# A sub-norm's scale spread over partitions: by way of DRAM, or by products with the identity

## The chip, the cores and the metric

One core of one Trainium2 chip runs the whole kernel. The metric is the device time of one execution in microseconds (us), as the median of several runs. The engines are named as in the profile: PE is TensorE, with PEld its weight loads, DVE is VectorE, ACT is ScalarE, POOL is GpSimd, and SP is SyncE, which issues the weight transfers. Each engine works through its own instructions in the order in which they stand.

## The reference, cut to what matters

Two layers run over 256 tokens of width 2048 in float32: a layer whose mixer is a convolution, then one whose mixer is a differential attention with 16 heads, each followed by a feed-forward part with a short convolution. The change lies in the attention, between the value product of a head and the output projection:

```python
a = p[:, :, 0] - lam * p[:, :, 1]
return jnp.einsum('bhqk,bkhe->bqhe', a.astype(v.dtype), v)
...
o = _rmsnorm(o, subln_g) * (1.0 - lambda_init)
return o.reshape(B, S, D_MODEL) @ w_o
```

So each head's output of 128 channels is divided, token by token, by the root of the mean of its squares, before it is multiplied by the learned gain and goes into `w_o`.

## The kernel before, in words

Activations lie with channels on the 128 partitions and the 256 tokens along the free dimension. A matrix product takes weights from DRAM in tiles of 128 x 1024 (512 KB), one tile a step (L183, `run`). Each tile is split by `split_w` into a rounded part `hi` (ACT, L150) and the rest `lo` (DVE, L152, or POOL), and PE multiplies `hi` with both parts of the activation (L226, 512 columns) and `lo` with the first (L227, 256 columns). That is one pair of products; a step of the query/key and output products is eight such pairs. The tiles are split four steps ahead of their use, and up to five raw tiles are on their way.

Work that follows a product is put off by a number of steps with `self.at(delay, fn)`, so that other products lie between a piece of work and what it waits for. The order on each engine comes from the program order, as shifted by a scheduler of the language, and is fixed when the kernel is built.

The attention (`attention`) runs over 16 heads. Before every fourth head stands a group of eight steps that makes the values of four heads (`v_group`, L774 to L776). Then come four steps for each head's query and key (`qk_post`, with the addition L256, the multiplication L795, the splits L263 and L264 and POOL's copy G at L801). Scores (L819, L822) and softmax follow two steps later, transposes (L847) four after that, the value product (`av`, L856 to L859) three after that. `av` writes the PSUM tile `o`; ACT copies it to SBUF and squares it (L862, L864). Two steps later `subln` sums the squares over the channels on PE (L274, `chan_sums`), which leaves one value for each token with the tokens on partitions; DVE scales them (L285) and POOL takes the power -0.5 (L286, tile `c`).

To multiply the head's output, this value must stand in every partition with the tokens along the free dimension. Heads 0 to 13 do that by way of DRAM: L878 writes the 256 values to the DRAM tile `rd`, and L879 reads them back into all 128 partitions, as the SBUF tile `M`. Both are issued from ACT's queue, and L879 can only be issued when L878's transfer has landed. Three steps later `subln2` multiplies (DVE, L886) and splits the result for the output projection (L267, L268). Heads 14 and 15 use `rows` instead (L280): two products with the identity matrix, whose stationary side is the column `c` repeated 128 times, write the values into all partitions of a PSUM tile, `o` or `t`.

The PSUM tag `o` is one bank with one buffer, `t` likewise, `s` has two; the large products use `pp`. A tile of a tag with one buffer can be written only when the reader of the tile before it has finished.

The output projection takes the heads' outputs as its inner dimension, 16 products of 128 channels for each pair of output tiles. The last head's products are held back for the first pairs.

Of the kernel before, what the change touches and what calls it, by code (L numbers as in the profile page):

```python
# [8 lines left out]
F32 = mybir.dt.float32  # L9
# [5 lines left out]
P = 128  # L15
S = 256
# [9 lines left out]
class Cfg:  # L26
    """Shapes; everything follows from the model width and the FFN width."""

    def __init__(self, d, f, kc=4):
        self.D, self.F = d, f  # L30
        self.KT = d // P
        self.FT = f // P
        self.H = d // (2 * HD)
        self.KC = kc
        self.NW = kc * 256
        self.kcs = [(i, kc) for i in range(0, self.KT, kc)]
        full = self.KT // 2
        first = self.FT % full or full
        self.chunks = [(0, first)] + [(i, full) for i in range(first, self.FT, full)]
        self.VK = kc // 2  # L40
        self.NA, self.NB = self.KT + self.KT // 2 + 1, 8
        # taps of the 31-tap convolution that go to the tensor engine, in fours, by channel tile
        self.G = [2] * (self.KT - 5) + [3, 3, 5, 6, 0]
        # the last tile's taps go there one by one
        self.ND = 18
# [16 lines left out]
class Builder:  # L62
# [25 lines left out]

    # temporaries; a tag's tiles are handed out in program order, so what runs late has tags of its own
    def b2(self, tag, dt=F32):  # L90
# [21 lines left out]

# [1 line left out]
    def act_tile(self, dt=F32R):  # L114
# [18 lines left out]

# [1 line left out]
    def load_w(self):  # L135
# [20 lines left out]
    def ahead(self, i):  # L156
        """weight tiles up to i split, some more on their way"""
        N = len(self.W)
        while self.ns < min(N, i + 1):
            while self.np_ < min(N, self.ns + 5):  # L160
                self.load_w()
            self.split_w()
# [38 lines left out]

# [1 line left out]
    def pair(self, wsrc, off, ksub, src, post, lo="v", pre=None, held=None, merged=False, halves=None):  # L203
        """halves(): two banks of [P, 512] instead of one tile of two;
        ksub: [(k0, nk)]; src(k) -> activation slot; held: a list that takes the last k instead of a step"""
        nc = self.nc
# [43 lines left out]
    def summed(self, ps):  # L250
        """main + correction halves -> [P, 2, S] in SBUF"""
        nc = self.nc
        cs = self.b2("E")
        nc.scalar.copy(cs, ps[:, :, S:])  # L254
        t = self.b2("E")
        nc.vector.tensor_tensor(t, ps[:, :, 0:S], cs, ALU.add)  # L256
        return t

    def split_act(self, dst, src, scale=None, num=None):
        """dst [P, 2, S] f32r <- hi and lo of src*scale (scale: [P, 1] pointer, or num: an exact number)"""  # L260
        nc = self.nc
        if scale is None and num is None:
            nc.scalar.copy(dst[:, 0, :], src)  # L263
            nc.vector.tensor_tensor(dst[:, 1, :], src, dst[:, 0, :].bitcast(F32), ALU.subtract)  # L264
        else:
            sc = num if scale is None else scale
            nc.scalar.activation(dst[:, 0, :], src, AF.Copy, scale=sc)  # L267
            nc.vector.scalar_tensor_tensor(dst[:, 1, :], src, sc, dst[:, 0, :].bitcast(F32), ALU.mult, ALU.subtract)  # L268

# [1 line left out]
    def chan_sums(self, ps, srcs):  # L271
# [5 lines left out]
    def rows(self, ps, col):  # L277
        """ps [P, S] <- col [P, 2] with tokens along the free dim, in every partition"""
        for t in range(2):
            self.nc.tensor.matmul(ps[:, t * P:(t + 1) * P], col[:, t:t + 1].to_broadcast([P, P]), self.ident,  # L280
                                  start=True, stop=True)
# [5 lines left out]

# [1 line left out]
    def new_norm(self, gname, goff, final=False):  # L289
# [49 lines left out]
    def norm_rows(self, st):  # L339
        ps = self.psx("o", [P, S])  # L340
        self.rows(ps, st["rc"])
        st["rows"] = ps
        if st["final"]:
            # the vector engine reads one copy in PSUM, GpSimd another by way of SBUF
            ps = self.psx("t", [P, S])
            self.rows(ps, st["rc"])
        st["rstd"] = self.const.tile([P, S], F32, tag="rstd", name=self.nm("rstd"), bufs=2)
        self.nc.scalar.copy(st["rstd"], ps)
# [6 lines left out]

# [1 line left out]
    def x_add(self, ps, pr, bias=None, merged=False):  # L357
# [66 lines left out]

# [1 line left out]
    def conv_module(self, nin, nout):  # L426
        c, a = self.c, self.a
# [5 lines left out]
        def post(i, ps):  # L433
# [11 lines left out]
            if i == KT - 1:  # L445
                self.at(0, lambda: last_taps(u, dgl))
                return
            # four shifted copies of 32 channels each, by way of DRAM: [(shift, channel), block, token]
            g = c.G[i]
# [11 lines left out]
            if i == 0:  # L461
                # diagonal weights of the last tile's taps on the tensor engine
                for j in range(0, c.ND, 4):
                    t = self.b2("Y" if j < 16 else "A").rearrange("p a (b s) -> p (a b) s", b=2)[:, :min(4, c.ND - j), :]
                    n = t.shape[1]
                    nc.gpsimd.tensor_tensor(t, self.ident.unsqueeze(1).to_broadcast([P, n, P]),
                                            self.col("cw", (KT - 1) * CK + j, n).unsqueeze(2).to_broadcast([P, n, P]), ALU.mult)
                    dgl.extend(t[:, x, :] for x in range(n))
# [10 lines left out]
        def last_taps(u, dgl):  # L479
            """the last tile: taps on both engines at once, in sums of their own"""  # L480
            i = KT - 1
# [24 lines left out]
        def tap_step(n=6):  # L506
            """some taps on the vector engine, two tiles by turns so that none waits for the one before it"""
            while chains and n > 0:
# [21 lines left out]
        def shift(c0):  # L530
            """per-token shift: the mean of the first tile; it cancels in the normalisation"""
            ps = self.psx("o", [P, S])
# [45 lines left out]
        def layernorm():  # L578
# [44 lines left out]
            with self.tc.manual_schedule(engines={ET.DVE, ET.Activation, ET.Pool}):  # L623
# [8 lines left out]
                for i in range(KT):  # L632
                    # a vector-engine pair is normalised at least one pair ahead of its use
                    while todo and 2 * todo[0][0] + todo[0][1] <= i + 2:
                        norm(*todo.pop(0))
                    act(i)
                    if todo and i >= 1:
                        norm(*todo.pop(0))
                    low(i)
# [17 lines left out]

# [1 line left out]
    def ffn(self, layer, nin, nout, begin=None):  # L659
# [57 lines left out]

# [1 line left out]
    def attn_setup(self):  # L719
        """relative bias by distance, one sheared copy per query row in DRAM; lambda"""  # L720
        nc, c, a = self.nc, self.c, self.a
# [27 lines left out]
    def attention(self, nin, nout):  # L749
# [63 lines left out]
        def scores(h, q, k, qk):  # L813
            bm = bias(h)
            ps = [self.psx("s", [P, 2, S]) for _ in range(2)]
            # the first 128 queries see the first 128 keys only: one float32 product costs less than three of 256 columns
            comp = [slice(cc * HD, (cc + 1) * HD) for cc in range(2)]
# [49 lines left out]
        def subln(h, o, sq):  # L867
# [3 lines left out]
            self.rsqrt_cols(rc, ps[:, 0:4:2], 1.0 / P)  # L871
            if h >= H - 2:
                self.at(2, lambda: subln2(h, o, rc, None))
                return
            # to every partition by way of DRAM
            rd = self.dr.tile([S], F32, tag="rd", name=self.nm("rd"), bufs=3)
            rr = self.b1("M")
            nc.scalar.dma_start(rd.rearrange("(t p) -> p t", p=P), rc)  # L878
            nc.scalar.dma_start(rr, rd.unsqueeze(0).to_broadcast([P, S]))  # L879
            self.at(3, lambda: subln2(h, o, rc, rr))  # L880

        def subln2(h, o, rc, rr):
            if rr is None:
                rr = self.psx("t" if h == H - 1 else "o", [P, S])
                self.rows(rr, rc)
            nc.vector.tensor_tensor(o, o, rr, ALU.mult)  # L886
# [64 lines left out]
def _onehot(np):  # L951
    """bucket of each distance key - query = j - 255"""
    oh = np.zeros((NB, 384), np.float32)
# [8 lines left out]
def layout(cfg, inp):  # L962
    """host side: repacking only"""
    import numpy as np
# [79 lines left out]
```

## Time and profile before

| | |
|---|---|
| median of 3 runs | 2394.99 us (2393.94 to 2396.80) |
| span of the profiled execution | 2415.1 us |
| PE busy | 2255.2 us, 93% of the span |
| DVE busy | 1667.8 us, 69% |
| ACT busy | 1201.8 us, 50% |
| POOL busy | 283.3 us, 12% |
| DMA | 419.02 MB, mean 174 GB/s |

The profile is of one execution, and its span runs from the first to the last instruction; it is 20.1 us longer than the median of the runs, which were taken without a profile. No other time of that execution is given. A busy share is an average over stages with different limits, so the stretch where the attention runs, about 1138 to 1606 us of the span, has to be read by itself. A wait names the instruction that ended it. The granted clock is a share of 2.4 GHz: 1.00, or 0.50, which is 1.2 GHz.

### The profile page before, as it was taken

Reading aid. Unit: us, or ns where it says so; the run is one execution under the profiler, and the core shown is the slowest. Engines: PE = TensorE matmul, PEld = TensorE weight load, DVE = VectorE, ACT = ScalarE, POOL = GpSimd, SP = SyncE. Lnnn points to the kernel's source line nnn. Section 1 sums busy time; section 2 is a strip of 40 time slices with the busy share of each in tenths; the row PEclk is TensorE's granted clock in tenths of the full one; section 3 lists DMA queues with packets and bytes.
Section 4 is the critical chain, followed back from the end, with each engine's and each line's share of the span. In section 5 each row is a group of like instructions: output and inputs, shape, how many; then the busy total and the mean of one; then the engine's idle time right before and its main releaser. Section 6 shows DMA issues by size and latency. Waiting matters only on the chain. (4 is left out here: it accounts for less than half of the span.)

```text
span 2415.1 us, 34577 instructions
## 1 busy us (share of the span) xinstructions
PE 2255.2 (93%) x13238; PEld 1968.0 (81%) x13238; DVE 1667.8 (69%) x2539; ACT 1201.8 (50%) x1788; POOL 283.3 (12%) x189
## 2 busy tenths in 40 slices
PE   6999799899999999999978776889999999999998
PEld 6888688788888888888867665778888888888887
DVE  5888874777767677778646363667777767676774
ACT  4333363655545455556534343455555555454554
POOL 5678410000000000001101000110000000000002
PEclk8999899899999999999988888899999999999999
DMA  6766267666666666666655545555666666666663
GB/s 227 196 186 189 78 197 185 191 187 191 189 189 186 190 190 188 190 185 190 181 98 142 121 124 104 132 155 183 188 188 186 191 186 189 191 185 191 185 190 105
DMA packets 132711, 419.02 MB, mean 174 GB/s; under 512 B 18208, under 2 KB 34112, under 8 KB 132544
## 3 DMA queue, kind: packets, MB, share of 16 engines
q1 hardware_dynamic: 110736, 398.30, 55.7%
q10 hardware_dynamic: 21808, 18.51, 4.0%
q8 instruction: 104, 1.70, 0.3%
q14 instruction: 63, 0.52, 0.1%
HBM read 409.27 MB, written 7.47 MB: 173 GB/s over the span
## 5 line engine op out<-in xcount | busy, mean ns | idle before, releaser
L226 PE MATMUL pp<-act,hi 128*128 128x512 f32 x3902 | 1393.8, 398 | 28.8 <-DVE E L256 13.2
L227 PE MATMUL pp<-act,lo 128*128 128x256 f32 x3902 | 1101.6, 282 | 0.0
L150 ACT CAST hi<-raw 128x1024 fp32r<-128x1024 f32 x752 | 787.4, 1049 | 550.2 <-issue 172.2
L152 DVE TENSOR_TENSOR lo<-raw,hi 128x1024 fp32r<-128x1024 f32 x686 | 844.0, 1231 | 260.9 <-ACT hi L150 259.9
L226 PEld LDWEIGHTS pp<-act,hi 128*128 128x128 f32 x3902 | 739.1, 189 | 193.3 <-DVE E L256 13.5
L227 PEld LDWEIGHTS pp<-act,lo 128*128 128x128 f32 x3902 | 745.0, 191 | 10.3 <-issue 0.7
L226 PE MATMUL pp<-actb,hi 128*128 128x512 f32 x856 | 309.7, 399 | 0.0
L227 PE MATMUL pp<-actb,lo 128*128 128x256 f32 x856 | 241.8, 283 | 0.0
L217 PE MATMUL pp<-act,hi 128*128 128x256 f32 x1088 | 210.1, 295 | 11.3 <-ACT act L267 6.2
L321 POOL TENSOR_TENSOR ssq<-ssq,Z 128x512 f32<-128x512 f32 x24 | 35.5, 1481 | 1530.9 <-ACT Z L317 1530.8
L217 PEld LDWEIGHTS pp<-act,hi 128*128 128x128 f32 x1088 | 178.9, 201 | 20.7 <-DVE act L268 6.3
L226 PEld LDWEIGHTS pp<-actb,hi 128*128 128x128 f32 x856 | 162.3, 190 | 38.9 <-issue 0.6
L256 DVE TENSOR_TENSOR E<-pp,E 128x512 f32<-128x512 f32 x104 | 72.0, 692 | 164.2 <-ACT E L254 163.8
L254 ACT COPY E<-pp 128x512 f32<-128x512 f32 x104 | 60.9, 586 | 231.5 <-PE pp L224 170.6
L152 POOL TENSOR_TENSOR lo<-raw,hi 128x1024 fp32r<-128x1024 f32 x66 | 159.3, 2432 | 59.1 <-ACT hi L150 54.0
L227 PEld LDWEIGHTS pp<-actb,lo 128*128 128x128 f32 x856 | 163.2, 191 | 0.3 <-issue 0.2
L217 PE MATMUL pp<-act,lo 128*128 128x256 f32 x544 | 158.4, 291 | 2.8 <-DVE lo L152 2.8
L370 ACT COPY E<-pp 128x512 f32<-128x512 f32 x109 | 64.1, 588 | 168.7 <-PE pp L224 161.1
L677 DVE SCALAR_TENSOR_TENSOR Y<-fpad,prm,Y 128x256 f32<-128x256 f32 x352 | 147.0, 480 | 0.0
L372 DVE TENSOR_TENSOR x<-pp,x 128x512 f32<-128x512 f32 x101 | 69.9, 692 | 88.6 <-ACT E L370 88.1
L674 ACT ACTIVATE Y<-fpad,prm 128x256 f32<-128x256 f32 x176 | 96.3, 595 | 48.2 <-DVE fpad L670 48.2
L513 DVE SCALAR_TENSOR_TENSOR s<-cpad,cprm,s 128x256 f32<-128x256 f32 x214 | 97.5, 482 | 23.3 <-PE s L475 21.0
(219 smaller groups left out, 1912.8 us busy)
## 6 DMA issues: line engine op xcount, KB each, us to landing
raw<-in_w_up_dram SPq DMA_DIRECT2D x352, 512.0 KB, 3.9
raw<-in_w_down_dram SPq DMA_DIRECT2D x176, 512.0 KB, 3.9
raw<-in_w_in_dram SPq DMA_DIRECT2D x64, 512.0 KB, 4.5
raw<-in_w_qk_dram SPq DMA_DIRECT2D x64, 512.0 KB, 4.3
raw<-in_w_out_dram SPq DMA_DIRECT2D x32, 512.0 KB, 4.2
raw<-in_w_v_dram SPq DMA_DIRECT2D x32, 512.0 KB, 3.7
raw<-in_w_o_dram SPq DMA_DIRECT2D x32, 512.0 KB, 3.8
R<-ud ACTq DMA_DIRECT2D x44, 130.0 KB, 5.3
```

The costliest lines, as they stand in the source:

```text
L150: nc.scalar.copy(hi[:, :n], raw[:, :n])
L152: eng.tensor_tensor(lo[:, :n], raw[:, :n], hi[:, :n].bitcast(F32), ALU.subtract)
L217: nc.tensor.matmul(ps[:, 0:S], w[:, kk, cs], xt[:, x, :], start=(k == first and n == 0), stop=(k == last and n == 2))
L226: nc.tensor.matmul(*main, start=(k == first), stop=False)
L227: nc.tensor.matmul(*corr, start=False, stop=False)
L254: nc.scalar.copy(cs, ps[:, :, S:])
L256: nc.vector.tensor_tensor(t, ps[:, :, 0:S], cs, ALU.add)
L370: nc.scalar.copy(cs, ps[:, :, S:])
L372: nc.vector.tensor_tensor(x, ps[:, :, 0:S], x, ALU.add)
L513: nc.vector.scalar_tensor_tensor(acc, u[:, j:j + S], self.col("cw", i * CK + j), acc, ALU.mult, ALU.add)
L674: nc.scalar.activation(y[:, j, :], u[:, j, FK - 1:], AF.Identity, scale=self.col("fw", ch * FK + FK - 1), bias=self.col("fb", ch))
L677: nc.vector.scalar_tensor_tensor(y[:, j, :], u[:, j, q:q + S], self.col("fw", ch * FK + q), y[:, j, :], ALU.mult, ALU.add)
```

## The change

All 16 heads take the way that heads 14 and 15 took: the two transfers and the tiles `rd` and `M` are gone from `subln`, and `subln2` makes the scale with `rows`, always two steps after the sums.

```diff
             self.rsqrt_cols(rc, ps[:, 0:4:2], 1.0 / P)
-            if h >= H - 2:
-                self.at(2, lambda: subln2(h, o, rc, None))
-                return
-            # to every partition by way of DRAM
-            rd = self.dr.tile([S], F32, tag="rd", name=self.nm("rd"), bufs=3)
-            rr = self.b1("M")
-            nc.scalar.dma_start(rd.rearrange("(t p) -> p t", p=P), rc)
-            nc.scalar.dma_start(rr, rd.unsqueeze(0).to_broadcast([P, S]))
-            self.at(3, lambda: subln2(h, o, rc, rr))
-
-        def subln2(h, o, rc, rr):
-            if rr is None:
-                rr = self.psx("t" if h == H - 1 else "o", [P, S])
-                self.rows(rr, rc)
+            self.at(2, lambda: subln2(h, o, rc))
+
+        def subln2(h, o, rc):
+            rr = self.psx("t" if h == H - 1 else "o", [P, S])
+            self.rows(rr, rc)
             nc.vector.tensor_tensor(o, o, rr, ALU.mult)
```

The diff also drops comments and docstrings elsewhere; they move line numbers only (L886 is L877 in the changed kernel). The order of instructions on the engines shifts too. The names in the rows below are tiles with buffer numbers: `rd` and `M` as above, `E` a sum of two halves, `hi`, `lo` and `raw` weight tiles, `Y` the split query and key, `O` a head's output or its squares, `c` the column of scales, `at` and `au` the transposed weights of the attention, `act` and `actb` activations, `pp`, `o` and `s` PSUM tiles.

ACT, where head 0's scale is ready, about where the second value group begins; first the kernel before:

```order
L878 DMA rd_11689<-c_11685 128x2x1
L254 COPY E_11715<-pp_11568 128x512
L150 CAST hi_11762<-raw_11594 128x1024
L879 DMA M_11690<-rd_11689 128x256
L150 CAST hi_11828<-raw_11660 128x1024
L263 CAST Y_11720<-E_11717 128x256
L263 CAST Y_11721<-E_11717 128x256
L862 COPY O_11756<-o_11751 128x256
L864 ACTIVATE O_11758<-o_11751 128x256
L267 ACTIVATE act_11786<-O_11590,subg 128x256
```

and the changed one:

```order
L254 COPY E_11711<-pp_11568 128x512
L150 CAST hi_11765<-raw_11594 128x1024
L150 CAST hi_11827<-raw_11660 128x1024
L263 CAST Y_11716<-E_11713 128x256
L263 CAST Y_11717<-E_11713 128x256
L862 COPY O_11752<-o_11747 128x256
L864 ACTIVATE O_11754<-o_11747 128x256
```

The two transfers are gone from between the copy and the casts, and with L879 the point where ACT had to see L878's transfer landed.

DVE at the same place, before:

```order
L152 TENSOR_TENSOR lo_11763<-raw_11594,hi_11762 128x1024
L886 TENSOR_TENSOR O_11590<-O_11590,M_11690 128x256
L152 TENSOR_TENSOR lo_11829<-raw_11660,hi_11828 128x1024
L264 TENSOR_TENSOR Y_11720<-E_11717,Y_11720 128x256
L264 TENSOR_TENSOR Y_11721<-E_11717,Y_11721 128x256
```

and changed:

```order
L152 TENSOR_TENSOR lo_11766<-raw_11594,hi_11765 128x1024
L152 TENSOR_TENSOR lo_11828<-raw_11660,hi_11827 128x1024
L264 TENSOR_TENSOR Y_11716<-E_11713,Y_11716 128x256
L264 TENSOR_TENSOR Y_11717<-E_11713,Y_11717 128x256
L152 TENSOR_TENSOR lo_11853<-raw_11689,hi_11852 128x1024
L264 TENSOR_TENSOR at_3963<-t_11781,at_3963 128x256
L877 TENSOR_TENSOR O_11590<-O_11590,o_11756 128x256
L829 SCALAR_TENSOR_TENSOR Z_11803<-s_11791,bm_11788 128x128
```

The multiplication of head 0's output stands five rows later, behind two more weight splits and three activation splits, and reads the PSUM tile `o` that the identity products write.

PE at the tenants of the bank `o`, in the third value group, with most other products left out (one row of the scores, L819, is kept for the place); before, heads 5, 5, 6, 6 and 7:

```order
L856 MATMUL o_12596<-at_3965,act_11736 128x256
...
L819 MATMUL s_12637<-G_12567 128x128
...
L274 MATMUL o_12689<-ones,O_12603 128x2 x2
...
L856 MATMUL o_12736<-at_3963,act_11737 128x256
...
L274 MATMUL o_12792<-ones,O_12743 128x2 x2
...
L856 MATMUL o_12860<-at_3965,act_11738 128x256
```

and changed, heads 5, 4, 5, 6, 5, 6 and 7:

```order
L856 MATMUL o_12588<-at_3965,act_11732 128x256
...
L819 MATMUL s_12632<-G_12559 128x128
...
L280 MATMUL o_12597<-ident,c_12526 128x128 x2
...
L274 MATMUL o_12684<-ones,O_12595 128x2 x2
...
L856 MATMUL o_12727<-at_3963,act_11733 128x256
...
L280 MATMUL o_12736<-ident,c_12687 128x128 x2
...
L274 MATMUL o_12786<-ones,O_12734 128x2 x2
...
L856 MATMUL o_12850<-at_3965,act_11734 128x256
```

Between a value product and the sums of its own squares now stands the scale of the head before, in the same bank. In the changed order 26, 24, 20, 22, 24 and 20 other products stand in the six gaps.

## Rows read from the trace of the kernel before

**Rows 1.** The page's 40 slices of 60.4 us: PE's busy tenths, granted clock.

```profile
PE   6999799899999999999978776889999999999998
PEclk8999899899999999999988888899999999999999
```

**Rows 2.** Windows: length, busy us of each engine, PEclk, DMA share, GB/s.

```profile
1138.00:1212.00 74.00, 74.00 (x412) 62.44 (x411) 50.78 (x94) 40.20 (x76) 8.73 (x9) 1.00 0.60 181
1296.00:1332.00 36.00, 36.00 (x211) 30.38 (x209) 26.66 (x63) 18.41 (x44) 4.04 (x7) 1.00 0.55 142
1212.00:1324.00 112.00, 88.74 (x440) 73.17 (x439) 57.67 (x125) 44.65 (x98) 9.41 (x12) 0.86 0.52 122
1210.00:1606.00 396.00, 309.16 (x1582) 257.45 (x1581) 199.50 (x430) 155.64 (x336) 31.82 (x41) 0.86 0.52 119
```

**Rows 3.** DVE's waits, 1210 to 1606: us in total, times, longest.

```profile
DVE O L886 <- DMA M<-rd: 93.7, 14, 12.4
DVE E L256 <- ACT E L254: 36.5, 11, 13.4
```

**Rows 4.** L878, first transfer: who waited longest for it, and time to landing.

```profile
  ACT E L254: 35.7, 3
...
DMA to landing us min/median/max: 8.6/9.6/12.6
```

**Rows 5.** L879, second transfer: time to landing.

```profile
DMA to landing us min/median/max: 2.9/5.2/6.8
```

**Rows 6.** Timeline of head 0: start, us, engine, line, [idle before <-releaser].

```profile
1210.83 0.38 ACTq L878 DMA_DIRECT2D rd<-c  x1
...
1220.60 0.34 ACTq L879 DMA_DIRECT2D M<-rd  x1
...
1221.04 1.04 ACT L150 CAST hi<-raw 128x1024 fp32r<-128x1024 f32 x1 [7.18 <-PE s L819]
...
1226.25 0.42 DVE L886 TENSOR_TENSOR O<-O,M 128x256 f32<-128x256 f32 x1 [10.41 <-DMA M<-rd]
```

**Rows 7.** Timeline of PE in undisturbed products: two neighbouring pairs' starts.

```profile
1100.30 0.40 PE L226 MATMUL pp<-act,hi 128*128 128x512 f32 x1
...
1100.65 0.40 PE L226 MATMUL pp<-act,hi 128*128 128x512 f32 x1
```

**Rows 8.** PE's waits, 1210 to 1606: us in total, times, longest.

```profile
PE s L819 <- POOL G L801: 24.5, 3, 9.5
PE o L274 <- ACT O L864: 23.4, 6, 8.0
PE s L822 <- DVE Y L264: 20.6, 7, 6.4
...
PE o L856 <- DVE c L285: 1.5, 2, 0.9
```

**Rows 9.** Windows of the 12 stretches at low clock: first, last, sum.

```profile
1224.06:1234.30 10.24, 6.55 (x21) 5.14 (x20) 7.58 (x17) 2.92 (x5) 0.69 (x1) 0.51 0.76 154
...
1575.64:1585.88 10.24, 6.78 (x23) 6.01 (x24) 6.52 (x16) 4.55 (x11) 0.69 (x1) 0.51 0.38 110
sum 109.23, PE 64.97 PEld 53.91 DVE 71.11 ACT 47.20 POOL 7.44; mean PE 5.41 PEld 4.49 DVE 5.93 ACT 3.93 POOL 0.62
```

**Rows 10.** Chain that ended last, 1586 to 1590: the identity products of head 14.

```profile
1588.22 0.44 PE o L280 x4
```

**Rows 11.** L886 by where it reads: ns min/median/max.

```profile
L886 DVE TENSOR_TENSOR O<-O,M x14: 424/426/427, 1226.3 to 1577.0; 128x256 f32<-128x256 f32 x14
L886 DVE TENSOR_TENSOR O<-O,o x1: 414/414/414, 1589.4 to 1589.4; 128x256 f32<-128x256 f32 x1
```

**Rows 12.** Timeline of ACT after another first transfer.

```profile
1332.76 0.71 ACT L263 CAST Y<-E 128x256 fp32r<-128x256 f32 x2 [6.63 <-DMA rd<-c]
...
1334.32 0.36 ACT L862 COPY O<-o 128x256 f32<-128x256 f32 x1
1334.59 0.39 ACT L864 ACTIVATE O<-o 128x256 f32<-128x256 f32 x1
```

## Prediction

> **What bounds the kernel now.** I began with the busy tenths in slices: TensorE (PE) is full nearly everywhere, except in a few slices near the start and in one trough of seven slices past the middle, and the granted clock dips there too [rows 1]. The windows then say where that trough lies: while the first value group and the first four query/key pairs run (1138 to 1212 us), PE is busy for 74.00 of 74 us at clock 1.00; the next stretch of the same length of program takes 112 us, with PE busy for 88.74 at 0.86; and over 1210 to 1606 us PE is busy for 309.16 of 396.00 us [rows 2]. So TensorE is the bound outside the trough, and inside it something else is. 86.8 us of idleness lie there.
>
> Who waits for whom: VectorE (DVE) stands 93.7 us, 14 times, before L886 for the transfer that brings the scale back from DRAM, and nothing else makes it wait half as long [rows 3]. ScalarE (ACT) stands too: the second transfer is issued from its queue, must wait until the first has landed, and whatever comes behind it on that engine waits along. The first transfer lands 9.6 us after issue (median), and the group that waits longest behind it lost 35.7 us [rows 4]; the second needs 5.2 us more [rows 5]. One head shows the whole chain [rows 6]: the first transfer goes out at 1210.83; ACT's next cast starts at 1221.04 after 7.18 us idle (the row names PE's L819, which ended last; what stood ahead of the cast is L879, issued at 1220.60); DVE reaches L886 and stands 10.41 us, until 1226.25. Three steps of delay were meant to hide this, but a pair of products starts every 0.35 us [rows 7], a step is eight pairs, 2.8 us, and three steps are 8.4 us against 9.6 + 5.2 = 14.8 us.
>
> PE's own waits carry none of these names. They are for GpSimd's copy G (24.5 us), for ACT's square O (23.4), for DVE's Y (20.6), and less for others [rows 8]. I take them for the same stall at second hand: G, Y, the softmax and the split of O all pass through DVE behind L886, and the square is behind the transfer on ACT. What speaks for it: until the first L886 PE is never idle, and after DVE has caught up PE is full again at clock 1.00, 36.00 of 36 us from 1296 to 1332, with scores, softmax, transposes and value products running [rows 2].
>
> **The change part by part.**
>
> *Removed: 14 pairs of transfers and the waits on them.* All 86.8 us of PE's idleness go if my reading holds. Beside it goes the slow clock: within the trough there are 12 stretches (first, last and sum stand in [rows 9]) of 109.23 us at 0.5, the 1.2 GHz level; each begins in or right after a halt of PE and ends after it has been running again. PE is busy in them for 64.97 us, and at 2.4 GHz that work takes half, so 32.5 us more come back if no halts are left. The traffic itself is nothing.
>
> *Added: two products with the identity for each of 14 heads.* Heads 14 and 15 have them already: the two show as four passes that take 0.44 us of the chain at full clock [rows 10]. 14 x 0.44 = 6.2 us, on PE, which is the bound, so all of it counts.
>
> *Moved: where L886 (now L877) reads.* From PSUM it takes 414 ns, from SBUF 426 [rows 11]: nothing. It is put two steps behind the sums now, not three; DVE waits there for PE instead of for a queue.
>
> *The new wait: one bank for three tenants.* Value product, sums and scale share the bank "o", so each head now makes the chain: value product, ACT's copy and square, scale of the head before, DVE's multiplication, sums, DVE's L285, next value product. Three turns for each of 14 heads, 42 in all; at each PE waits if the reader is late, and everything behind waits with it. In the new order 20 to 26 other products stand between two tenants, which is 10 to 13 pairs or 3.5 to 4.5 us of cover at 0.35 us a pair. The readers need 0.36 + 0.39 us on ACT [rows 12] or some 0.4 us on DVE, and ACT and DVE are busy for only 40.20 and 50.78 us of the 74 us when PE is full [rows 2]. If the cover were gone, each turn would cost up to what the rows show for such turns. The bounds are nothing (the 36 us without a gap) and 0.75 us a turn (the two waits of L856 on L285, 1.5 us together [rows 8]), 42 x 0.75 = 31.5 us. I take 5 us, near the lower end, because the undisturbed stretches have no gap at all and the readers have slack.
>
> A rule of the Trainium skill speaks against the change here. The page "TensorE: Matmul & The Clock Gate", section "A second HAM failure mode: psum-queue depth-cycling", reports a kernel that cycles through PSUM banks, where PE idles briefly between groups and the clock swings between its levels. By that rule the low clock would stay, its 32.5 us would not be won, and the sum would come to some 2320 us, an estimate; this case's trace has it at 1.00 in the stretch where one bank "o" already had two tenants [rows 2], which does not test three.
>
> *What is late next.* Nothing that I can see: TensorE itself.
>
> **Sum.** 86.8 + 32.5 - 6.2 - 5 = 108.1 us, say 108. The profiled span is 2415.1 us, 20.1 us above the median of the runs, 2394.99. I carry the difference over unchanged: 2395 - 108 = **2287 us**. If the whole 20.1 us were longer stalls that only the profile has, the gain would be 88 us, and 2307. With no loss at the bank the gain is 113 us, 2282; 4 us below that allow for the spread of the three runs (2393.94 to 2396.80) and for rounding. So the forecast's own range is 2278 to 2307.
>
> **The rivals.**
>
> *The bank turns are felt.* Each of 42 turns costs 0.75 us: 2395 - 113 + 31.5 = 2313, from 2307 to 2335 if some clock is lost. For it: three tenants, in-order engines, casts of about 1.04 us on ACT ahead of a square [rows 12]. Against it: the cover above.
>
> *Half the stall had other causes.* DVE now waits at L877 for PE to come to the scale, with splits of weights queued behind it; or GpSimd's G is late by itself. Half of idleness and slow clock would stay: 2395 - 113 + (86.8 + 32.5)/2 = 2341. Against it: 93.7 us of DVE's waiting is more than PE's whole idleness.
>
> *Slower: PE stands at the bank as long as it has stood for a square.* L274 waited for ACT's square six times, 23.4 us, so 3.9 us each, 8.0 at most [rows 8]. Did every turn cost that, 42 x 3.9 = 164 us would come in: 2395 - 113 + 164 = 2446. It decides from 113/42 = 2.7 us a turn on. Against it: where I looked, ACT came to copy and square after 6.63 us lost behind the first transfer [rows 12], which the change takes away.
>
> *The transfers were hidden anyway.* Then only the products are added, 2395 + 6.2 = 2401, or less if a little is saved. The waits in [rows 3] and the idle time in [rows 6] speak flatly against it. The Trainium skill's page "DMA: Bandwidth & Descriptors" has a rule that would make it so: a transfer has a fixed cost of some 2.0 us plus its bytes. By that the pair would take an estimated 4.3 us, well inside three steps. The trace does not agree: 9.6 and 5.2 us [rows 4, 5], and the measurement decides.
>
> **How the numbers follow.** Forecast 0.80, felt bank turns 0.12, half the stall 0.04, the slower bank 0.02, hidden transfers 0.02. The range 2278 to 2315 holds the forecast's range and the middle of the first rival. A measurement of this kernel can tell 0.2% from no change, 4.8 us: the first three cases are faster, 0.96; of the hidden transfers half is within that, 0.01; the rest is slower, 0.03.
>
> **What would show it.** Right: the slices of the trough read 9 for PE and 9 for the clock; no L886 or L877 among DVE's long waits; PE's waits between the value groups and the output projection under 10 us in all; 2.4 GHz from 1138 us to the end of attention; a group of four heads takes about 80 us, not the 112 of [rows 2] (a quarter or so of the 108 us is won in each). Wrong: PE waiting at L280, L274 or L856 for ACT or DVE 40 times over (the bank), a new long wait of DVE for L280 with splits late behind it, or G still late with ACT and DVE free.

## The result and the profile after

The changed kernel takes **2301.97 us** (median of 4 runs, 2294.92 to 2305.00) beside 2395.48 us for the kernel before (4 runs, 2393.94 to 2396.80): a ratio of 0.9609, 95% interval 0.9594 to 0.9624, or 93.5 us less. The prediction said 2287 us, 2278 to 2315, and faster at 0.96.

The page of the changed kernel: span, busy times, and the 40 slices (57.5 us each) of PE's busy tenths and of the granted clock, the answer to [rows 1].

```profile
span 2300.4 us, 34637 instructions
PE 2224.6 (97%) x13294; PEld 1947.9 (85%) x13294; DVE 1670.9 (73%) x2539; ACT 1205.7 (52%) x1788; POOL 281.4 (12%) x189
...
PE   6899799799999999999999999999999999999998
...
PEclk9999899899999999999999999999999999999999
```

The trough of seven slices is gone from both. DVE, ACT and POOL do what they did; PE's busy time fell by 30.6 us (2255.2 to 2224.6) although 56 passes were added, because what it had done at the slow clock is now done at the full one.

Windows of the changed kernel, columns as in [rows 2], here one for each group of four heads:

```profile
1210.00:1290.00 80.00, 80.00 (x458) 67.49 (x457) 58.98 (x124) 45.40 (x95) 7.71 (x12) 1.00 0.55 165
1290.00:1370.00 80.00, 80.00 (x459) 67.49 (x458) 58.80 (x124) 45.64 (x99) 8.68 (x12) 1.00 0.55 165
1370.00:1450.00 80.00, 80.00 (x461) 67.56 (x461) 59.10 (x127) 45.82 (x98) 8.51 (x11) 1.00 0.54 164
1450.00:1510.00 60.00, 59.66 (x360) 51.94 (x359) 43.21 (x72) 34.14 (x62) 9.09 (x7) 1.00 0.52 157
```

PE is full and at 2.4 GHz in each. A value group's first product marks where four heads begin, and the three starts in PE's timeline lie 79.85 and 79.71 us apart, not the 112 us of [rows 2]:

```profile
1209.79 0.40 PE L774 MATMUL pp<-hi,act 128*128 128x512 f32 x1
...
1289.64 0.39 PE L774 MATMUL pp<-hi,act 128*128 128x512 f32 x1
...
1369.35 0.40 PE L774 MATMUL pp<-hi,act 128*128 128x512 f32 x1
```

These are all of PE's waits in the changed kernel between 1130 and 1510 us (us in total, times, longest), the answer to [rows 8]:

```profile
PE s L819 <- POOL G L801: 0.9, 1, 0.9
PE pp L226 <- DVE x L372: 0.3, 1, 0.3
```

And DVE's, of the same stretch, the answer to [rows 3]; L877 is the old L886:

```profile
DVE lo L152 <- ACT hi L150: 62.5, 58, 3.4
DVE c L285 <- PE o L274: 7.2, 11, 1.4
...
DVE O L877 <- PE o L280: 4.2, 9, 0.8
```

DVE's 93.7 us before L886 have become 4.2 us before L877 at bank `o`, and 1.7 us once at `t`, which the view lists further down. The 62.5 us for ACT's `hi` are 58 waits of about 1 us in an engine that has time to spare, and no PE wait follows from them.

### The profile page after: what moved, and what is told of

The parts are those of the page before. It is cut to its first block, busy times and chain, and to the rows that moved or that the text cites. A ratio compares the mean times of both kernels' runs of the same rounds, so it can differ in the third digit from the quotient of the medians.

```text
span 2300.4 us, 34637 instructions
## 1 busy us (share of the span) xinstructions
PE 2224.6 (97%) x13294; PEld 1947.9 (85%) x13294; DVE 1670.9 (73%) x2539; ACT 1205.7 (52%) x1788; POOL 281.4 (12%) x189
## 4 chain that ended last, share of the span: by engine, by line
PE 88%; DMA 5%; DVE 4%; issue 1%; ACTq 0%; ACT 0%; POOL 0%; POOLq 0%; SPq 0%; DVEq 0%
PE pp L226 47%; PE pp L227 24%; PE pp L224 4%; PE pp L217 3%; PE pp L223 2%; DMA R<-ud 2%; DMA ud<-cpad 2%; DMA d<-Z 2%; PE pp L774 1%; PE pp L775 1%; PE pp L776 1%; DVE s L513 1%; DVE cpad L440 1%; PE s L475 0%; ACTq L456 0%
```

## The experiments

Three questions were put: is it the waiting or the transfers that cost the time; which of the two waits (VectorE's for the scale, ScalarE's for the first landing); and what do the added products and the shared bank cost. The experiments were run on later occasions than the first comparison, on three chips, each group with runs of the kernel before beside it, which took 2409 to 2412 us (medians) on each of the three.

### The two kernels again

> The kernel before, unchanged. The profiled execution of before had a span of 2415.1 us, 20 us above the median of the runs, while the changed kernel's had 2300.4 against a median of 2302. If the profile itself lengthens the transfers by way of DRAM, the span is again some 20 us above the runs, 2410 to 2418, and the waits of L886 are again 90 to 95 us. If that one execution was an outlier, the span is 2391 to 2396 and the waits of L886 are some 20 us shorter.

Measured: 2412.85 us (10 runs), beside 2411.65 us (13 runs): 1.0002, interval 0.9988 to 1.0016. The profiled execution took 2415.31 us, span 2413.3, and the nine others 2404.08 to 2417.46. So a profiled execution is one among the others, and a span lies some 2 us under its time.

> The kernel before, unchanged, for one more profile beside the runs of this call. If it stands near 2395 us here, the first transfer lands sooner than the 9.6 us median of the trace shown, by 1 us or more a head, and L886 waits 70 to 80 us instead of 94; near 2412 us it waits 90 to 95 us again.

Measured: 2408.24 us, span 2406.3; DVE's wait at L886 was 88.6 us, 14 times, a little under the 90 to 95 expected at such a time.

> The changed kernel, unchanged, on the same chip as a run of the kernel before. The forecast's sum of 108 to 113 us came from a trace with a span of 2415.1 us; the first comparison had the kernel before at 2395 us and a gain of 93.5. If the kernel before differs from chip to chip by how long its transfers take and the changed one doesn't, the changed kernel is at 2298 to 2306 us wherever the kernel before stands, so the gain is about 110 us beside a before of 2412 and about 94 beside one of 2395.

Measured: 2304.62 us (2302.43 to 2305.03) beside 2409.04: ratio 0.9568 (0.9554 to 0.9581), a gain of 104.4 us. The changed kernel stands where it stood (2301.97); the kernel before is 14 us slower than in the first comparison.

### Half the heads by way of DRAM

```diff
-            if h >= H - 2:
+            if h % 2 == 1 or h >= H - 2:
```

> Heads 0, 2, 4, 6, 8, 10 and 12 go by way of DRAM, the other nine by products with the identity. Theory (each pair of transfers makes a stall of its own): half of the gain, 2395 - 93/2 = 2348 us, 2336 to 2360. Rival (a pair costs only because the pair of the head before it is still in the queue): most of the gain, below 2325. Rival (one slow pair a group is enough to hold everything): little of it, above 2375.

Measured: 2348.26 us (2346.90 to 2354.86), ratio 0.9740 (0.9723 to 0.9758). Its largest PE waits and the DVE wait, 1130 to 1600 us:

```profile
PE o L274 <- ACT O L864: 16.9, 4, 5.9
PE s L822 <- DVE Y L264: 9.9, 3, 4.2
PE s L822 <- ACT Y L263: 6.9, 3, 3.2
```

```profile
DVE O L886 <- DMA M<-rd: 49.1, 7, 11.2
```

Each pair of transfers stalls by itself: DVE waits 7.0 us a head (49.1 / 7; before, 93.7 / 14 = 6.7). What is left of the loss is 2348.26 - 2304.62 = 43.6 us for seven heads, 6.2 us each, somewhat less than the 104.4 / 14 = 7.5 us a head of the kernel before.

### Both transfers kept, both waits put off

The second transfer goes out seven steps after the first, the multiplication two steps after that; both are held in the program's order, because the scheduler otherwise moves them up. For the longer life of the tiles the square uses the tag `G`, `rd` has four buffers, and the last four heads use identity products.

```diff
-            if h >= H - 2:
+            if h >= H - 4:
...
-            nc.scalar.dma_start(rr, rd.unsqueeze(0).to_broadcast([P, S]))
-            self.at(3, lambda: subln2(h, o, rc, rr))
+            self.at(7, lambda: subln1(h, o, rc, rd))
+
+        def subln1(h, o, rc, rd):
+            rr = self.b1("M")
+            self.tc.keep_in_program_order(nc.scalar.dma_start(rr, rd.unsqueeze(0).to_broadcast([P, S])))
+            self.at(2, lambda: subln2(h, o, rc, rr))
```

> Heads 0 to 11 go by way of DRAM as before, but ACT issues the second transfer some 16 of its instructions after the first and DVE multiplies correspondingly later; the last four heads use the products with the identity; the squares lie in other buffers. The number and size of the transfers of these heads is unchanged. Theory (the engines' waits cost the time, not the transfers): nearly the changed kernel's time, 2290 to 2315 us. Rival (the transfers themselves, or their traffic beside the weights): 2370 to 2395.

Measured: 2303.38 us (2301.93 to 2311.26), ratio 0.9556 (0.9537 to 0.9575), the changed kernel's time. All of PE's waits, 1130 to 1610 us, then DVE's at the multiplication (L889 here), then the landings of the first transfer:

```profile
PE s L819 <- POOL G L801: 3.2, 2, 2.3
PE pp L226 <- DVE x L372: 0.3, 1, 0.3
```

```profile
DVE O L889 <- DMA M<-rd: 14.7, 7, 3.7
```

```profile
DMA to landing us min/median/max: 8.6/9.2/11.6
```

The transfers are as slow as before (9.2 us for the first, in [rows 4] 9.6; the second takes 8.5 us at the median, in [rows 5] 5.2) and run for 12 heads, and the time is gone all the same. So **the transfers cost nothing that these runs can tell; the loss came from the engines that stood for them.**

### One wait taken away, and then the other

First the product alone is put off, from three steps to nine and held there, with the second transfer still issued right behind the first (the rest as in the experiment above). VectorE then no longer stands, ScalarE does.

```diff
-            self.at(3, lambda: subln2(h, o, rc, rr))
+            self.at(9, lambda: subln2(h, o, rc, rr))
```

> As the run with both put off, but ACT issues the second transfer right behind the first, as in the kernel before; only DVE's multiplication is put off. So DVE finds the scale landed, and ACT still stands until the first transfer has landed. If DVE's wait alone makes the loss: 2290 to 2315 us. If ACT's wait makes a loss of its own, as the ACT waits of 109 us in the trace of before suggest: 2330 to 2375, with PE waiting for ACT's casts and squares. If ACT's wait makes all of it: 2380 and above.

Measured: 2360.46 us (2356.80 to 2361.12), ratio 0.9783 (0.9768 to 0.9797). ACT's longest wait and PE's, 1130 to 1610 us:

```profile
ACT E L254 <- DMA rd<-c: 49.4, 5, 11.6
```

```profile
PE s L819 <- POOL G L801: 26.9, 6, 7.1
PE o L274 <- ACT G L864: 11.0, 3, 4.3
```

About half of the loss is left, 2360.46 - 2304.62 = 55.8 us for 12 heads. I read this as two parts that add up: ScalarE's wait some 55 us, VectorE's the other 50. The mirror of it had to show that: the transfers issued from SyncE's queue, nothing put off, so that only VectorE stands.

```diff
-            nc.scalar.dma_start(rd.rearrange("(t p) -> p t", p=P), rc)
-            nc.scalar.dma_start(rr, rd.unsqueeze(0).to_broadcast([P, S]))
+            nc.sync.dma_start(rd.rearrange("(t p) -> p t", p=P), rc)
+            nc.sync.dma_start(rr, rd.unsqueeze(0).to_broadcast([P, S]))
```

> The kernel before with both transfers of heads 0 to 13 issued from SyncE's queue, ScalarE's no longer; nothing is put off. ScalarE then waits for no landing, VectorE still waits at L886. Theory A: the waits of ScalarE and VectorE each cost their own part of the loss of some 105 us; putting off the product alone (VectorE's wait gone, ScalarE's left) won about 50, so this, the mirror of it, wins about 55: 2345 to 2370 us with the kernel before at 2410; VectorE waits some 60 to 95 us at L886, and no ScalarE wait names rd. Rival B: ScalarE's wait is only there because VectorE's is, so freeing ScalarE alone gives nothing: 2400 to 2415. Rival C: SyncE now waits for the first landing (9.6 us a head) with the loads of weights queued behind it, and the casts come late: 2400 to 2440, with ScalarE or PE waiting for weights (raw).

Measured: 2406.19 us (2400.83 to 2411.12) beside 2409.69, ratio 0.9986 (0.9969 to 1.0004). Nothing was won, and **my reading of two parts that add was wrong**. VectorE did not stand the 60 to 95 us expected, but longer than before:

```profile
DVE O L886 <- DMA M<-rd: 148.0, 14, 12.7
```

The landings were no slower for it: 9.2 and 4.9 us at the median, 9.4 and 4.9 in the kernel before (run again). What VectorE no longer waits for is ScalarE: its waits for ScalarE's `E` and `act` were 39.9 + 29.6 us there and are 2.9 + 4.4 us here, so over the 14 heads it comes to L886 sooner and stands there for the same landing. All three waits together are 161.4 us there and 155.3 us here. What happened is seen at head 0. The kernel before (run again), rows of ACT's timeline, of DVE's and of PE's:

```profile
1218.85 0.34 ACTq L879 DMA_DIRECT2D M<-rd  x1
...
1221.11 0.38 ACT L864 ACTIVATE O<-o 128x256 f32<-128x256 f32 x1
1225.31 0.51 ACT L267 ACTIVATE act<-O,subg 128x256 fp32r<-128x256 f32 x1 [3.82 <-DVE O L886]
```

```profile
1224.85 0.43 DVE L886 TENSOR_TENSOR O<-O,M 128x256 f32<-128x256 f32 x1 [10.18 <-DMA M<-rd]
...
1226.33 0.75 DVE L264 TENSOR_TENSOR Y<-E,Y 128x256 fp32r<-128x256 f32 x2
```

```profile
1220.99 0.38 PE L822 MATMUL s<-Y,Y 64*128 64x256 f32 x2 [1.40 <-ACT Y L263]
...
1227.13 0.79 PE L822 MATMUL s<-Y,Y 64*128 64x256 f32 x4 [3.84 <-DVE Y L264]
```

The same rows with the transfers on SyncE's queue:

```profile
1215.80 0.39 ACT L864 ACTIVATE O<-o 128x256 f32<-128x256 f32 x1
1224.67 0.51 ACT L267 ACTIVATE act<-O,subg 128x256 fp32r<-128x256 f32 x1 [8.48 <-DVE O L886]
```

```profile
1224.21 0.42 DVE L886 TENSOR_TENSOR O<-O,M 128x256 f32<-128x256 f32 x1 [9.48 <-DMA M<-rd]
...
1225.69 0.75 DVE L264 TENSOR_TENSOR Y<-E,Y 128x256 fp32r<-128x256 f32 x2
```

```profile
1226.49 0.80 PE L822 MATMUL s<-Y,Y 64*128 64x256 f32 x4 [5.25 <-DVE Y L264]
```

ACT's square runs 5.31 us earlier (1221.11 to 1215.80), and then ACT waits 8.48 us where it waited 3.82: it comes to the split L267, which needs L886. DVE starts L886 0.64 us earlier, for that is set by the two landings, and `Y`, for which PE waits, is behind it. PE had halted twice, 1.40 us for ScalarE's part of `Y` and 3.84 us for VectorE's; now it halts once, 5.25 us for VectorE's, and goes on 0.64 us earlier. Over the attention PE's waits change their names and keep their size, 68.3 us in these two rows and 68.5 us in the first three of [rows 8]:

```profile
PE s L822 <- DVE Y L264: 46.6, 7, 9.0
PE pp L226 <- ACT vu L788: 21.7, 3, 9.6
```

So the waits of a head lie beside each other, and the one that ends last, VectorE's, sets the pace. The same from GpSimd's queue (as above, with `nc.gpsimd`):

> The same from GpSimd's queue, which has no weight loads. GpSimd then waits for the first landing, and its copies G (L801) and powers of the reciprocal roots (L286) stand behind that. Theory A: as from SyncE, 2345 to 2370 us. Rival B: 2400 to 2415. Rival C, the wait goes with the queue: GpSimd's copy G comes late, PE waits at L819 for G 40 us or more in all, and the time is 2375 to 2420.

Measured: 2416.58 us (2410.88 to 2423.16), ratio 1.0028 (1.0015 to 1.0041). One row of POOL's waits and one of PE's:

```profile
POOL M L879 <- DMA rd<-c: 127.7, 14, 9.9
```

```profile
PE s L819 <- POOL G L801: 26.4, 8, 5.5
```

The wait for the first landing stands on whichever engine issues the second transfer. PE's wait for `G` stayed below the 40 us expected of that case, and VectorE stood 157.4 us at L886, as in the run before this one. The rise of 0.3% is small beside the rest.

If waits that lie beside each other are the rule, both edits together must free PE:

> Both edits together: the transfers are issued from SyncE's queue, the second right behind the first, and VectorE's multiplication is put off by nine steps (heads 0 to 11 by DRAM, the last four by identity products). Theory A as it was, parts that add (50 for VectorE, and nothing for ScalarE by the last run), would give 2360 us, as with ScalarE's queue. Theory D: the two waits of a head lie beside each other and end PE's work at nearly the same time, so that taking one away leaves the other to set the pace, and only both together free PE: 2300 to 2315 us, PE waits under 10 us between 1130 and 1510 us, no L886 among VectorE's waits over 15 us, and SyncE's waiting for the first landing (some 9 us a head) costs nothing, since raw weights are loaded five tiles ahead. Rival C: SyncE's wait makes the weights late: 2330 to 2400.

Measured: 2311.37 us (2307.37 to 2313.87) beside 2411.11, ratio 0.9593 (0.9572 to 0.9615). PE's waits, 1130 to 1510 us; then a row of SyncE's queue and one of ACT's:

```profile
PE t L847 <- DVE A L841: 4.3, 5, 1.0
PE s L819 <- POOL G L801: 4.0, 4, 2.0
PE pp L226 <- DVE x L372: 0.3, 1, 0.3
```

```profile
SPq L879 <- DMA rd<-c: 123.4, 12, 12.3
```

```profile
ACT hi L150 <- DMA raw<-in_w_qk_dram: 45.0, 21, 5.7
```

It came out so, within the 2300 to 2315 us expected. SyncE stands 123.4 us for the landings with the weights behind it, and ACT meets some of them late (45.0 us), but PE hardly does. The four cases:

| | VectorE waits | VectorE does not |
|---|---|---|
| **ScalarE waits** | 2409 to 2412 (before) | 2360.46 |
| **ScalarE does not** | 2406.19 | 2311.37; 2303.38 with both put off |

Taking ScalarE's wait away wins nothing while VectorE's stands, and 49 us (2360.46 - 2311.37) once it is gone.

The two columns are not quite alike: on the left 14 heads go by way of DRAM, on the right 12. The groups of four heads that begin with the second and the third value group go by way of DRAM in all of these runs, and their lengths, from L774's first product to that of the next group, set this right:

| us from group to group | second | third |
|---|---|---|
| before | 112.26 | 109.33 |
| transfers from SyncE's queue | 111.07 | 108.78 |
| product put off | 98.39 | 101.70 |
| SyncE's queue, product put off | 85.74 | 79.79 |
| both put off | 78.01 | 77.61 |

So with ScalarE's wait alone not half but two thirds of the loss is left in these groups, 44.5 of 66.0 us over the two; with VectorE's alone all but 1.7 us of it. What the way over SyncE's queue costs beside putting both off lies mostly in one group (85.74 beside 78.01).

### The price of the products and of the bank

```diff
-            self.rows(rr, rc)
+            for _ in range(3):
+                self.rows(rr, rc)
```

> The changed kernel with the two identity products of every head made three times over into the same tile, so 32 more pairs of products. Theory (TensorE is the bound through the attention, and each added product counts in full at 0.44 us a head): 2 x 16 x 0.44 = 14 us slower than the changed kernel, 2313 to 2320. Rival (there is room on TensorE between waits): within 5 us of the changed kernel. If the bank is held longer and its turns are felt: 2325 and above.

Measured: 2314.74 us (2312.54 to 2315.36), 10.1 us above the changed kernel's 2304.62 beside it, for 32 more pairs of products (16 heads, two more each). By these medians a pair would cost 0.32 us, but they hold the whole kernel: in the profiled executions alone the attention begins at 1133.01 us here and at 1134.79 and 1135.35 us in the two of the changed kernel. The attention by itself is clearer. The first products of its value groups:

```profile
1207.49 0.40 PE L774 MATMUL pp<-hi,act 128*128 128x512 f32 x1
...
1291.14 0.40 PE L774 MATMUL pp<-hi,act 128*128 128x512 f32 x1
...
1374.78 0.40 PE L774 MATMUL pp<-hi,act 128*128 128x512 f32 x1
```

They lie 83.65 and 83.64 us apart, 3.8 and 3.9 us more than in the changed kernel (79.85 and 79.71), for eight more pairs in each group: **0.48 us a pair**. The run with both waits put off says the same from the other side: there these groups have no identity products, and take 1.8 and 2.1 us less (78.01 and 77.61) for four pairs. All of PE's waits, 1130 to 1510 us:

```profile
PE s L819 <- POOL G L801: 0.9, 1, 0.9
PE pp L226 <- DVE x L372: 0.3, 1, 0.3
```

The two rows are those of the changed kernel. The scale takes three times as many passes in bank `o`, and still PE waits for no reader there.

### Sums and spread in one product

To do without identity products, one float32 product with a matrix of ones leaves the sums in all partitions at once; DVE scales them, and GpSimd takes the power on all 128 x 256 values, where the changed kernel has 128 x 2.

```diff
...
-            self.chan_sums(ps, [sq])
-            rc = self.c2()
-            self.rsqrt_cols(rc, ps[:, 0:4:2], 1.0 / P)
...
+            nc.tensor.matmul(ps, self.ones, sq, start=True, stop=True)
+            rr = self.b1("M")
+            nc.vector.tensor_scalar(rr, ps, 1.0 / P, EPS, ALU.mult, ALU.add)
+            nc.gpsimd.tensor_tensor(rr, rr, self.mhalf[:, 0:1].to_broadcast([P, S]), ALU.pow)
...
```

> The changed kernel with sums and spread in one: a float32 product of a full matrix of ones with the 128 x 256 squares leaves the sum in every partition, DVE scales it from the bank into SBUF, GpSimd takes the power of 128 x 256 values, and the identity products fall away. So the bank o has two tenants a head. TensorE saves 0.34 + 0.44 us a head and pays about 0.44, some 5 us in all: 2293 to 2300 us. Rival (GpSimd's power of 256 columns takes several us and delays its copies G, which the scores wait for): above 2305.

Measured: 2688.85 us, ratio 1.1163 (1.1147 to 1.1179), far from the 2293 to 2300 expected. POOL's group by line (busy time, mean ns of one), and DVE's wait for it:

```profile
L872 POOL TENSOR_TENSOR M<-M,mhalf 128x256 f32<-128x256 f32 x16 | 657.6, 41108 | 8.8 <-DVE smx L833 8.8
```

```profile
DVE O L876 <- POOL M L872: 308.1, 13, 39.2
```

One power takes 41.1 us, where the expectation's rival had several, and DVE stands for it as it stood for the transfers, only longer. No version that was run clearly beats the changed kernel.

## Why the prediction was right, and where it was off

**What bounded the kernel: shown, with one link that I had wrong.** DVE's waits at L886 are gone, and PE's waits for `G`, `O` and `Y`, which I took for the same stall at second hand, went with them: 24.5 + 23.4 + 20.6 us in [rows 8], 0.9 us after. I named both engines as the way by which the stall reached PE, and that holds; what I did not say is that they stand beside each other. The four cases show that VectorE's wait alone keeps nearly the whole loss. Since the change takes both away, the sum was not touched by this. One sign was misread: PE is not "never idle" until the first L886. Its first halt in that trace, 1.98 us for ScalarE's `Y`, ends at 1222.75 us, while VectorE still stands before L886 (until 1226.25); it belongs to ScalarE's wait. And the casts of 1.04 us, put down to [rows 12], stand in [rows 6].

**86.8 us of idleness and 32.5 us of slow clock: right for the profile before.** The windows after show PE full at clock 1.00. With the bank's term at nothing, 86.8 + 32.5 - 14 x 0.44 - 0 = 113.1 us, and the two profiled spans lie 2415.1 - 2300.4 = 114.7 us apart, those of the runs again 2413.3 - 2299.9 = 113.4 us.

**Identity products: 0.44 us a head, right within a tenth.** The lengths of the groups give 0.48 us a head, 14 x 0.48 = 6.7 us in place of 6.2.

**The bank's 42 turns: nothing, not 5 us.** No PE wait names bank `o`, not even with the scale's passes tripled. So the first rival, 2313 us by felt turns, is out, though its time was not far from what came, and so is the slower bank at 2446. The low clock that the rule of the Trainium skill on cycling PSUM banks would have left ("TensorE: Matmul & The Clock Gate", section "A second HAM failure mode: psum-queue depth-cycling", some 2320 us in the prediction) did not appear: three tenants shared one bank, and the four windows of the attention read clock 1.00. What the rule starts from, PE idling briefly between groups, did not come about either, so these runs do not test it.

**Half the stall with other causes: out.** L877 waits 4.2 + 1.7 us for PE, and PE waits for `G` once, 0.9 us.

**Hidden transfers: out.** The reading from the Trainium skill's page "DMA: Bandwidth & Descriptors", by which the pair would have stayed under three steps, fails in every run that kept the transfers: medians of 9.2 to 12.3 us for the first. The page (section "Anatomy of one DMA — SWDGE (gpsimd) path") gives its 2.0 us for transfers from GpSimd's queue, where those of the prediction's trace went from ScalarE's; the run from GpSimd's queue has 9.6 and 4.5 us for the two, so it does not agree there either.

**The base was the step that missed.** "I carry the difference over unchanged: 2395 - 108" takes a gain read from an execution of 2415.1 us of span and sets it against runs of 2395 us. The gain was 93.5 us there, and 104.4 us where the kernel before took 2409.04. The text had the right case as a bound ("the gain would be 88 us, and 2307"), but for a reason that does not hold: the profile does not lengthen the stalls, since the profiled executions of the kernel run again lie among the others. The execution read was a long one: its span of 2415.1 us lies near the top of the spans of all later runs, 2398.0 to 2416.7. The kernel before itself took 2394 to 2397 us in the first comparison and 2400 to 2419 in all later ones, on three chips, while the changed one moved only from 2301.97 to 2304.62. That it is the kernel with the stalls which moves fits stalls of another length, but no profile of before was taken among the 2395 us runs, on which chip they ran is not on record, and why they were shorter stays open. In part the forecast came close by luck: the 5 us for the bank, which cost nothing, made up for as much of the miss. Without it the same step gives 2282 us, 20 us below what was measured, about the 20.1 us by which the span exceeded the median.

## What to carry to other kernels

A transfer that is issued from a compute engine's queue and depends on another transfer makes that engine wait for a landing; look for whatever is queued behind it, and behind each instruction that reads the result, before you call the transfer hidden. When several engines wait for one latency, do not add up their waits or judge one cure alone: find the wait that ends last, and take them away together. A value that can be spread by two products of some 0.5 us together should not make a round trip of 14.8 us, unless its reader can be put off and held there; and a gain read from one profiled execution belongs to that execution's time. A small price is better read from a stretch of the trace that holds little else than from the medians of the whole kernel: 0.48 us a pair here, where the medians gave 0.32.

## What was not expected of the hardware

- The power on GpSimd: 41.1 us for 128 x 256 float32 values, where the 128 x 2 form in the changed kernel takes 0.69 us (row below): 128 times the columns for 60 times the time. Times of GpSimd are rough in the profile, but VectorE's longest wait for one, 39.2 us, bears this out.

```profile
L286 POOL TENSOR_TENSOR c<-c,mhalf x16: 689/691/1637, 1207.8 to 1479.9; 128x2 f32<-128x2 f32 x16
```

- SyncE, which issues all weights, stood 123.4 us between 1130 and 1510 us for the first landings, in the run with SyncE's queue and the product put off, with 8.6 us of PE waits in all.
- On SyncE's queue, with the product put off, the first transfer of 256 values took longer than on ScalarE's, 12.3 us at the median; on the same queue without the product put off it took 9.2 us, so the queue alone is not the cause, which stays open:

```profile
DMA to landing us min/median/max: 8.3/12.3/13.7
```
